# Moving the modulation columns to GpSimd's queue and re-tiling the first output projection

## The chip, the cores and the metric

The kernel runs on one core of a Trainium2 chip. The metric is the device time of one execution, in microseconds (us). Before the change three runs took 2764.96, 2761.36 and 2760.85 us, so the median is 2761.36 us.

A core has a matrix engine (TensorE, PE in the profile; its weight loads are PEld), a vector engine (VectorE, DVE), a scalar engine (ScalarE, ACT), GpSimd (POOL) and a sync engine (SyncE, SP) that issues transfers. Transfers between HBM and the on-chip memory are executed by 16 DMA engines, whoever issued them. Each engine works through its own instructions strictly in order; an instruction that waits holds everything behind it on that engine.

## The reference

Everything is float32, one batch entry, 512 tokens (S), model width 2048 (D). Two layers:

```python
mod = sc @ ada_w[l] + ada_b[l]            # sc = silu(c): one vector of 2048; mod: 3 x 2048 numbers
shift, scale, gate = mod[:, :D], mod[:, D:2*D], mod[:, 2*D:]
h = modulate(rmsnorm(x, g_pre[l]), shift, scale)
y = mlstm_mixer(h, ...)                    # layer 0: 8 heads, width 4096, then @ a_w_out (4096 x 2048)
# layer 1: hkv = modulate(rmsnorm(x, kv_g), ...); kv = hkv @ kv_w; band attention; @ b_w_out
x = x + gate * rmsnorm(y, g_post[l])
```

The `mod` numbers are matrix-vector products. The kernel computes them one "column" at a time: a tile of 128 partitions by 2048 numbers holds the weights of 128 outputs, and one VectorE instruction multiplies it with the broadcast `sc` and sums along the row.

## The kernel before, in words

**Weights.** All weights come as one stream of pieces in a fixed order (`stream`, L75). A piece is a tile of 128 x 1024 numbers, 512 KB. `raw_load` (L223) issues its load on SP into one of three raw buffers; `wpiece` (L232) splits the piece into a rounded part `wh` (a ScalarE copy) and a remainder `wl` (a VectorE subtraction, L213), and the products are made from three matrix multiplications, high x high, high x low, low x high (`mm3`, L280). The raw buffer is free for the next load once `wl` is made. So each piece passes SP, DMA, ScalarE, VectorE and TensorE in turn, with three raw buffers, three of `wh` and three of `wl`.

**Columns.** 32 columns (shift and scale of layer 0) are loaded and summed while the first projections start, on SP's queue. 48 more, 1 MB each, follow in the background while heads 0, 1 and the start of 2 are computed: `background(n)` (L743) first places the sums of the columns loaded by its previous call and then the loads of the next `n`, up to three, in two buffers `ada` of pool `ap_` and one of pool `bp`. Sums and loads are pinned, that is they keep their place in program order on VectorE and on SP. The 32 columns of layer 1's shift and scale come during layer 0's output projection, and the last of them during the key projection, as 64 half columns of 512 KB (`scale_step`, L1096: sums of two halves, then loads of the next two, in two buffers `adh`). They too are on SP's queue, in front of and behind weight pieces.

**Output projection of layer 0.** The result has four token blocks of 128 and four column groups of 512. `rows(g, ms, ...)` (L1065) computes column group `g` for the token blocks `ms`. A piece holds two of the 32 contraction steps of a group; it feeds 2 x 3 matrix multiplications for each token block, so 24 when all four blocks are computed together and 12 when two are. Before, group 0 is computed for all four blocks, then groups 1, 2, 3 for blocks 0 and 1, then groups 1, 2, 3 again for blocks 2 and 3: each of these three groups is loaded and split twice. While blocks 2 and 3 are computed, blocks 0 and 1 are finished: `residual` (L1010) adds the gated result to the input (loads `xr`, stores `xsc`), `turned` (L1030) transposes the normalised rows on TensorE into `ps_x` and stores them to `nsc`; later `kept` (L1056) reads them back from `nsc` and `key_input` (L1022) makes the input `hkv` of the key and value projection.

**Order.** A scheduler orders each engine's instructions by priority (weights are called ahead of their place by `high_priority`), except that pinned instructions stay in program order among themselves.

Of the kernel before, what the change touches and what calls it, by code (L numbers as in the profile page):

```python
# [74 lines left out]
def stream():  # L75
# [30 lines left out]
    for h in range(NH):  # L106
# [50 lines left out]
def hybrid_trunk(ctx, tc, xT, xN, c, adaT, cols, wst, wg, ext, kc, out):  # L157
# [74 lines left out]
    def wpiece(mat, groups=(), pl=None, bufs=(2, 2), early=False):  # L232
# [42 lines left out]
        return out  # L275

    def mm(ps, a, b, start, stop):
        return nc.tensor.matmul(ps, a, b, start=start, stop=stop)  # L278

# [213 lines left out]
    sp = st.enter_context(pool("start"))  # L493
    def ada_load(i, p, n, pin=lambda ins: ins, parts=1, js=None):

        w = D // parts
        js = range(parts) if js is None else js
        at = p.tile([P, w * len(js)], F32, tag="ada", name=f"ada{i}_{js[0]}", bufs=n)
        for j in js:
            c = (j - js[0]) * w  # L500
            pin(nc.sync.dma_start(at[:, c : c + w], adaT[i, :, j * w : (j + 1) * w]))
        return i, at, w, js
# [313 lines left out]
    for h in range(NH):  # L816
# [4 lines left out]
        for i in range(4):  # L821
            if h > HALF:
                if i % 2 == 0:
                    zs = pair((i // 2) * (V0 // 2) + h * DK, f"zq{h}_{i}", BANKS[i // 2])
                ps = zs[i % 2]
            elif h < 2:
                ps = (lead, qk1)[h][i]
            else:
                ps = newp(f"ps_qk{h}_{i}")
                proj_a("a_w_in", h1, ps)  # L830
            qk.append(conv(ps, chs[i], f"{h}_{i}", 1 < h <= HALF))
            if 1 < h <= HALF:
                background(2 - i % 2)
        zs = ps = None
# [52 lines left out]
        if h < HALF:  # L887
            background(2)
        if h:
            so = []  # L890
        for i in range(4):
# [7 lines left out]
            elif h:  # L899
                ps = newp(f"ps_o{h}_{i}")  # L900
                proj_a("a_w_in", h1, ps)
                so.append(acp.tile([P, S], F32, tag="so", name=f"so{h}_{i}", bufs=6))
                nc.scalar.activation(so[i], ps, AF.Sigmoid)
                background(2 - i % 2)
        for i in range(4):
# [41 lines left out]
        if h < HALF:  # L947
            background(3 if h == 0 else 1)
        if h == 3:
# [79 lines left out]

    def turned(pair, gs, use):  # L1030

        ms = PAIRS[pair]
        t = slice(2 * P * pair, 2 * P * (pair + 1))
        for g in gs:
# [5 lines left out]
            for kk in range(2):  # L1040
# [10 lines left out]
                nc.sync.dma_start(nsc[k : k + 2, :, t].rearrange("a p t -> p a t"), keep)  # L1051
                if use:
                    for j in range(2):
                        key_input(k + j, ps[:, j * 2 * P : (j + 1) * 2 * P], t)

# [8 lines left out]

    def rows(g, ms, xs, at={}):  # L1065
        ps = [newp(f"ps_y0_{g}_{m}") for m in ms]
        proj_b("a_w_out", xs, ps, ms=ms, kts=32, at=at)
        with tc.high_priority(AHEAD):
            for p, m in zip(ps, ms):
                yt[m].append(rp.tile([P, S], F32, tag="r", name=f"y{m}_{g}"))  # L1070
                evac(p, m, g, yt[m][g])

    scale_cols = [(48 + i, j) for j in range(2) for i in range(2 * KT)]
    scale_in, scH = [], []

    def scale_sums():

        for i, j, a in scale_in:
            pin(nc.vector.tensor_tensor_reduce(
                a, a, scH[j], 1.0, mod[:, i : i + 1] if j else col(CB + i), ALU.mult, ALU.add, mod[:, i : i + 1]  # L1080
            ))
        scale_in.clear()

    def scale_load():

        for i, j in scale_cols[:2]:
            d = slice(j * 2 * S, (j + 1) * 2 * S)
            if len(scH) == j:
                scH.append(cp.tile([P, 2 * S], F32, tag="sc", name=f"scH{j}"))
                pin(nc.sync.dma_start(scH[j], csc[0, d].partition_broadcast(P)))  # L1090
            a = cp.tile([P, 2 * S], F32, tag="adh", name=f"adh{i}_{j}", bufs=2)
            pin(nc.sync.dma_start(a, adaT[i, :, d]))
            scale_in.append((i, j, a))
        del scale_cols[:2]

    def scale_step():  # L1096
        scale_sums()
        scale_load()

    def scale_steps(*ks):  # L1100
        return {k: scale_step for k in ks}

    gate_row(0, 0)
    rows(0, range(4), y_tile, scale_steps(*range(2, 32, 4)))
    for pair, ms in enumerate(PAIRS):
        for g in range(1, 4):
            at = scale_steps(4, 12, 20, 28) if pair == 0 else {}
            if pair == 1 and g == 1:
                at = {2: lambda: residual(0), 4: lambda: residual(1)}
                at |= {20 + 4 * i: lambda i=i: turned(0, [i], False) for i in range(3)}  # L1110
            if pair == 1 and g == 2:
                at = {2: lambda: turned(0, [3], False)}
            if pair == 1 and g == 3:
                at = {k: lambda k=k: [key_input(i, kept(i, slice(0, 2 * P)), slice(0, 2 * P)) for i in range(k // 2 - 1, k // 2 + 1)] for k in range(2, 32, 4)}
            if pair == 1:
                add_at(at, scale_steps(*((8, 14, 18), (6, 14, 22), ())[g - 1]))
            gate_row(0, g)
            rows(g, ms, ys, at)

# [45 lines left out]
    for pair, ms in enumerate(PAIRS):  # L1165
        for g in range(2):
            turn = {2 + 4 * i: lambda i=i: turned(1, [i], True) for i in range(4)} if pair == 0 and g == 1 else {}
# [19 lines left out]
    assert not scale_cols and not scale_in  # L1187
    zxst.close()
    cqst.close()
    kst.close()  # L1190
# [281 lines left out]
```

## Time and profile before

| what | value |
|---|---|
| median of three runs | 2761.36 us |
| profiled execution | 2767.03 us |
| its span, first to last instruction | 2765.2 us |
| TensorE busy | 2734.7 us |
| VectorE busy | 2320.6 us |
| ScalarE busy | 1437.0 us |
| moved by DMA | 527.25 MB |

How to read it. A busy time counts an instruction from start to end; matrix multiplications overlap, so TensorE reads as busy even in short delays. The window view gives, for a stretch of time, the length, then the busy time and number of instructions of each engine (TensorE, its weight loads, VectorE, ScalarE, GpSimd), the granted TensorE clock, the mean busy share of the 16 DMA engines and the GB/s moved. The view of waits gives who waited for whom: total us, times, longest. The chain view follows the work that ended last back through what released it: start, duration, what. The view of transfers gives the line and tile, number of issues, KB each and the median us from issue to landing.

### The profile page before, as it was taken

Reading aid. Unit: us, or ns where it says so; the run is one execution under the profiler, and the core shown is the slowest. Engines: PE = TensorE matmul, PEld = TensorE weight load, DVE = VectorE, ACT = ScalarE, POOL = GpSimd, SP = SyncE. Lnnn points to the kernel's source line nnn. Section 1 sums busy time; section 2 is a strip of 40 time slices with the busy share of each in tenths; the row PEclk is TensorE's granted clock in tenths of the full one; section 3 lists DMA queues with packets and bytes.
Section 4 is the critical chain, followed back from the end, with each engine's and each line's share of the span. In section 5 each row is a group of like instructions: output and inputs, shape, how many; then the busy total and the mean of one; then the engine's idle time right before and its main releaser. Section 6 shows DMA issues by size and latency. Waiting matters only on the chain.

```text
span 2765.2 us, 45016 instructions
## 1 busy us (share of the span) xinstructions
PE 2734.7 (99%) x17554; PEld 2487.5 (90%) x17554; DVE 2320.6 (84%) x3694; ACT 1437.0 (52%) x2046; POOL 0.2 (0%) x4
## 2 busy tenths in 40 slices
PE   8999999999999999999999999999999999999998
PEld 6887887899999999999998877787998899999887
DVE  8978978989999899998988657667997788899666
ACT  4243523556556565565555234468435566666523
POOL 0000000000000000000000000000000000000000
PEclk9999999999999999999999999999999999999999
DMA  9757787333333233333338778988655544444687
GB/s 368 291 204 275 258 314 255 102 98 120 109 111 113 97 124 108 115 110 100 125 106 284 251 268 293 317 275 279 214 183 187 171 129 129 127 122 126 213 299 256
DMA packets 165296, 527.25 MB, mean 191 GB/s; under 512 B 17701, under 2 KB 33605, under 8 KB 154457
## 3 DMA queue, kind: packets, MB, share of 16 engines
q1 hardware_dynamic: 165082, 524.38, 56.3%
q8 instruction: 137, 2.24, 0.3%
q14 instruction: 77, 0.63, 0.1%
HBM read 490.69 MB, written 38.85 MB: 192 GB/s over the span
## 4 chain that ended last, share of the span: by engine, by line
PE 84%; DMA 7%; DVE 6%; issue 2%; ACT 1%; SPq 0%; DVEq 0%; ACTq 0%
PE ps_y L278 11%; PE ps_azo L278 5%; PE ps_czo L278 5%; PE ps_dzo L278 5%; PE ps_kv L278 4%; PE ps_v L278 4%; PE ps_az L278 3%; PE ps_cz L278 3%; PE ps_dz L278 3%; PE ps_l L278 3%; DMA wr<-in_wst 3%; PE ps_bzo L278 3%; PE ps_o L278 3%; PE ps_s L278 2%; PE ps_czq L278 2%; PE ps_cv L278 2%
## 5 line engine op out<-in xcount | busy, mean ns | idle before, releaser
L213 ACT CAST wh<-wr 128x1024 fp32r<-128x1024 f32 (+1 forms) x560 | 579.2, 1036 | 563.7 <-PE ps_y L278 159.8
L213 DVE TENSOR_TENSOR wl<-wr,wh 128x1024 fp32r<-128x1024 f32 (+1 forms) x560 | 671.2, 1203 | 164.8 <-ACT wh L213 163.4
L278 PE MATMUL ps_y<-wh,y 128*128 128x512 f32 x1536 | 478.0, 391 | 0.2 <-ACT sqy L1000 0.2
L213 ACT CAST wsh<-ws 128x768 fp32r<-128x768 f32 (+1 forms) x272 | 222.5, 818 | 406.1 <-issue 128.7
L278 PEld LDWEIGHTS ps_y<-wh,y 128*128 128x128 f32 x1536 | 288.9, 188 | 60.5 <-ACT sqy L1000 0.6
L213 DVE TENSOR_TENSOR wsl<-ws,wsh 128x768 fp32r<-128x768 f32 (+1 forms) x272 | 253.8, 933 | 91.0 <-ACT wsh L213 88.3
L278 PE MATMUL ps_y<-wl,y 128*128 128x512 f32 x768 | 301.7, 393 | 5.4 <-DVE wl L213 5.3
L507 DVE CUSTOM_DVE_ANT_0 ada<-ada,scB,cl 128x2048 f32<-128x2048 f32 (+1 forms) x80 | 185.2, 2319 | 22.8 <-DMA ada<-in_adaT 22.6
L252 DVE TENSOR_TENSOR ws<-wr 128x512 f32<-128x512 f32 (+1 forms) x272 | 181.0, 670 | 2.7 <-DMA wr<-in_wst 2.6
L278 PEld LDWEIGHTS ps_y<-wl,y 128*128 128x128 f32 x768 | 144.7, 188 | 41.8 <-DVE wl L213 12.1
L278 PE MATMUL ps_kv<-wh,hkv 128*128 128x512 f32 x512 | 159.6, 391 | 0.5 <-ACT wh L213 0.5
L278 PE MATMUL ps_v<-wh,h 128*128 128x512 f32 x384 | 120.2, 390 | 0.0
L278 PEld LDWEIGHTS ps_kv<-wh,hkv 128*128 128x128 f32 x512 | 96.1, 188 | 20.6 <-ACT wh L213 0.9
L254 DVE TENSOR_TENSOR ws<-wr 128x256 f32<-128x256 f32 (+1 forms) x272 | 111.0, 413 | 3.0
L253 DVE TENSOR_TENSOR wr<-ws,wr 128x256 f32<-128x256 f32 (+1 forms) x272 | 110.5, 411 | 1.9
L278 PE MATMUL ps_kv<-wl,hkv 128*128 128x512 f32 x256 | 100.0, 391 | 1.1 <-DVE wl L213 1.1
L278 PE MATMUL ps_l<-h,wh 128*128 128x512 f32 x320 | 98.4, 390 | 0.0
L278 PEld LDWEIGHTS ps_v<-wh,h 128*128 128x128 f32 x384 | 72.0, 188 | 14.8
L278 PE MATMUL ps_azo<-h,wh 128*128 128x256 f32 (+1 forms) x404 | 82.1, 294 | 0.0
L278 PE MATMUL ps_v<-wl,h 128*128 128x512 f32 x192 | 75.1, 391 | 0.0
L278 PEld LDWEIGHTS ps_l<-h,wh 128*128 128x128 f32 x320 | 59.9, 188 | 12.7 <-ACT wh L213 0.3
L278 PE MATMUL ps_dzo<-h,wh 128*128 128x256 f32 x364 | 69.6, 283 | 0.0
(442 smaller groups left out, 7219.4 us busy)
## 6 DMA issues: line engine op xcount, KB each, us to landing
wr<-in_wst SPq DMA_DIRECT2D x530, 512.0 KB, 3.9
ada<-in_adaT SPq DMA_DIRECT2D x78, 1024.0 KB, 7.1
adh<-in_adaT SPq DMA_DIRECT2D x64, 512.0 KB, 5.5
ada<-in_adaT SPq DMA_DIRECT2D x36, 512.0 KB, 6.1
xt<-nsc SPq DMA_DIRECT2D x48, 256.0 KB, 3.9
wr<-in_wst SPq DMA_DIRECT2D x26, 384.0 KB, 3.9
yr<-ysc SPq DMA_DIRECT2D x28, 256.0 KB, 5.3
ysc<-zo SPq DMA_DIRECT2D x24, 256.0 KB, 4.0
```

Of the source, the lines that this page charges most:

```text
L213: ins = nc.scalar.copy(hi, src), nc.vector.tensor_tensor(lo, src, hi.bitcast(F32), op=ALU.subtract)
L252: nc.vector.tensor_tensor(t[:, : 2 * w], r[:, w : 3 * w], r[:, : 2 * w], op=ALU.subtract)
L253: nc.vector.tensor_tensor(r[:, w : 2 * w], t[:, w : 2 * w], r[:, :w], op=ALU.add)
L254: nc.vector.tensor_tensor(t[:, 2 * w :], r[:, 3 * w :], r[:, w : 2 * w], op=ALU.subtract)
L278: return nc.tensor.matmul(ps, a, b, start=start, stop=stop)
L507: pin(nc.vector.tensor_tensor_reduce(c, c, (sc or scB)[:, j * w : (j + 1) * w], 1.0, mod[:, i : i + 1] if j else col(CB + i), ALU.mult, AL ...
```

## The change

1. `ada_load` takes the queue as an argument. `background` now issues its loads on GpSimd's queue, fills up to three loads on every call, and sums the `n` oldest instead of all; its calls are spread differently over heads 0 and 1. The 64 half columns move to GpSimd's queue too, with three buffers in place of two, three at a time.
2. A background sum is still pinned, and besides is placed behind the matrix multiplication that was last written when the call was made (`paced`). This is an ordering for the scheduler, and no wait on the chip.
3. The output projection of layer 0 computes groups 0 and 1 for all four token blocks, then groups 2 and 3 for blocks 0 and 1, then groups 2 and 3 for blocks 2 and 3. The stream has six groups of 16 pieces in place of seven.
4. The residual of blocks 0 and 1 is made during group 2 of the second pair, and all of `turned` during its group 3, where it makes the key input directly from `ps_x`. Reading it back from `nsc` falls away.
5. All half columns are summed by the end of the output projection, none in the key projection. The result tiles of group 3 of the first pair lie in the pool `tp`, of six buffers.

```diff
-    tile_b("a_w_out", 0, 32)
-    for _ in PAIRS:
-        for g in range(1, 4):
-            tile_b("a_w_out", g * 512, 32)
+    for g in (0, 1, 2, 3, 2, 3):
+        tile_b("a_w_out", g * 512, 32)
...
+    def paced(ins):
+        behind(ins, product[0])
+        return pin(ins)
+
     def background(n):
-        for a in loaded:
-            ada_sum(*a, tc.keep_in_program_order)
-        loaded.clear()
-        for b, i in enumerate(pending[:n]):
-            loaded.append(ada_load(i, *((ap_, 2) if b < 2 else (bp, 1)), tc.keep_in_program_order))
-        del pending[:n]
+        for a in loaded[:n]:
+            ada_sum(*a, paced)
+        del loaded[:n]
+        while pending and len(loaded) < 3:
+            p, bufs = (bp, 1) if len(pending) % 3 == 0 else (ap_, 2)
+            loaded.append(ada_load(pending.pop(0), p, bufs, pin, queue=nc.gpsimd))
...
-                background(2 - i % 2)
+                background(2)
...
-            add_at(at, {k: lambda: background(2) for k in ((2, 4, 6, 8, 10, 12, 14) if h == 0 else (2, 6, 12))})
+            add_at(at, {k: lambda: background(2) for k in ((0, 4, 8, 12) if h == 0 else (2, 6, 10, 14))})
...
+    def half_sums_step():
+        for i, j, a, w in halves:
+            paced(nc.vector.tensor_tensor_reduce(
+                a, a, w, 1.0, mod[:, i : i + 1] if j else col(CB + i), ALU.mult, ALU.add, mod[:, i : i + 1]
+            ))
+        halves.clear()
+        while cols_left and len(halves) < 3:
+            i, j = cols_left[0]
+            d = slice(j * 2 * S, (j + 1) * 2 * S)
...
+            a = cp.tile([P, 2 * S], F32, tag="adh", name=f"adh{i}_{j}", bufs=3)
+            pin(nc.gpsimd.dma_start(a, adaT[i, :, d]))
+            halves.append((i, j, a, sc[1]))
+            cols_left.pop(0)
...
     gate_row(0, 0)
-    rows(0, range(4), y_tile, scale_steps(*range(2, 32, 4)))
+    rows(0, range(4), y_tile, steps_at(*range(4, 32, 4)))
+    gate_row(0, 1)
+    rows(1, range(4), ys, steps_at(*range(0, 32, 4)))
     for pair, ms in enumerate(PAIRS):
-        for g in range(1, 4):
...
+        for g in (2, 3):
+            if pair == 0:
+                at = steps_at(*((4, 14, 24), (2, 12, 22))[g - 2])
+            elif g == 2:
+                at = {2: lambda: residual(0), 6: lambda: residual(1), 14: half_sums_step, 24: half_sums_step}
+            else:
+                at = {6 + 6 * i: lambda i=i: turned(0, [i]) for i in range(4)}
             gate_row(0, g)
-            rows(g, ms, ys, at)
+            rows(g, ms, ys, at, tp if pair == 0 and g == 3 else None)
...
-        if 0 < i < 7:
-            at[1] = scale_step
-        if i == 7:
-            at[1] = lambda: (scale_sums(), amul_cols(2, 48 + KT, GPRE + KT))
```

More of the change, by code (lines that the diff above doesn't have):

```diff
@@ L275, in wpiece @@
         return out
+    product = [None]
     def mm(ps, a, b, start, stop):
-        return nc.tensor.matmul(ps, a, b, start=start, stop=stop)
+        product[0] = nc.tensor.matmul(ps, a, b, start=start, stop=stop)
+        return product[0]
     def mm3(ps, ah, al, bh, bl, start, stop):
@@ L493, in hybrid_trunk, with ada_load @@
     sp = st.enter_context(pool("start"))
-    def ada_load(i, p, n, pin=lambda ins: ins, parts=1, js=None):
+    def ada_load(i, p, n, pin=lambda ins: ins, parts=1, js=None, queue=nc.sync):
         w = D // parts
@@ L500, in ada_load @@
             c = (j - js[0]) * w
[L501 removed]
+            pin(queue.dma_start(at[:, c : c + w], adaT[i, :, j * w : (j + 1) * w]))
         return i, at, w, js
@@ L1028, in key_input, with turned @@
         split(hkv[k][:, 0, t], hkv[k][:, 1, t], tmp)
-    def turned(pair, gs, use):
+    def turned(pair, gs):
         ms = PAIRS[pair]
@@ L1051, in turned @@
                 nc.sync.dma_start(nsc[k : k + 2, :, t].rearrange("a p t -> p a t"), keep)
-                if use:
-                    for j in range(2):
-                        key_input(k + j, ps[:, j * 2 * P : (j + 1) * 2 * P], t)
+                for j in range(2):
+                    key_input(k + j, ps[:, j * 2 * P : (j + 1) * 2 * P], t)
     def kept(k, t):
@@ L1063, in hybrid_trunk, with rows @@
     yt = [[] for _ in range(4)]
-    def rows(g, ms, xs, at={}):
+    def rows(g, ms, xs, at={}, pl=None):
         ps = [newp(f"ps_y0_{g}_{m}") for m in ms]
@@ L1069, in rows @@
             for p, m in zip(ps, ms):
-                yt[m].append(rp.tile([P, S], F32, tag="r", name=f"y{m}_{g}"))
+                yt[m].append((pl or rp).tile([P, S], F32, tag="t" if pl else "r", name=f"y{m}_{g}"))
                 evac(p, m, g, yt[m][g])
[L1073 to L1080, printed above, removed]
-            ))
-        scale_in.clear()
@@ L1084, in scale_load @@
-    def scale_load():
-        for i, j in scale_cols[:2]:
+    cols_left = [(48 + i, j) for j in range(2) for i in range(2 * KT)]
+    halves, sc = [], [None, None]
+    def half_sums_step():
+        for i, j, a, w in halves:
+            paced(nc.vector.tensor_tensor_reduce(
+                a, a, w, 1.0, mod[:, i : i + 1] if j else col(CB + i), ALU.mult, ALU.add, mod[:, i : i + 1]
+            ))
+        halves.clear()
+        while cols_left and len(halves) < 3:
+            i, j = cols_left[0]
@@ L1103, in hybrid_trunk, with steps_at @@
+    def steps_at(*ks):
+        return {k: half_sums_step for k in ks}
     gate_row(0, 0)
-    rows(0, range(4), y_tile, scale_steps(*range(2, 32, 4)))
+    rows(0, range(4), y_tile, steps_at(*range(4, 32, 4)))
+    gate_row(0, 1)
+    rows(1, range(4), ys, steps_at(*range(0, 32, 4)))
     for pair, ms in enumerate(PAIRS):
-        for g in range(1, 4):
[L1107 to L1116, printed above, removed]
+        for g in (2, 3):
[5 more added lines that the diff above has]
+                at = {6 + 6 * i: lambda i=i: turned(0, [i]) for i in range(4)}
@@ L1117, in hybrid_trunk @@
             gate_row(0, g)
-            rows(g, ms, ys, at)
+            rows(g, ms, ys, at, tp if pair == 0 and g == 3 else None)
+    assert not cols_left and not halves
+    amul_cols(2, 48 + KT, GPRE + KT)
+    cqst.close()
     def values(g, ms, at={}):
@@ L1166, in hybrid_trunk @@
         for g in range(2):
-            turn = {2 + 4 * i: lambda i=i: turned(1, [i], True) for i in range(4)} if pair == 0 and g == 1 else {}
+            turn = {2 + 4 * i: lambda i=i: turned(1, [i]) for i in range(4)} if pair == 0 and g == 1 else {}
             if pair:
```

25 lines of the change are left out of this document (8 added, 17 removed).

## The prediction

> **What bounds the kernel now.** I read the page's shares first, then the chain of work that ended last, then the window view of the stages that the chain leaves TensorE in, then the waits inside them.
>
> ```profile
> span 2765.2 us, 45016 instructions
> PE 2734.7 (99%) x17554; PEld 2487.5 (90%) x17554; DVE 2320.6 (84%) x3694; ACT 1437.0 (52%) x2046; POOL 0.2 (0%) x4
> ...
> PE 84%; DMA 7%; DVE 6%; issue 2%; ACT 1%; SPq 0%; DVEq 0%; ACTq 0%
> ```
>
> TensorE is the bound, and the change takes no matrix multiplication away. What can be won is where the chain leaves TensorE. It does so in the start, at the end of head 1 (between us 366 and 425) and in the output projection of layer 0 (us 1557 to 1757). GpSimd does nothing: its queue is free.
>
> The next rows are windows of the output projection, counting `ps_y` products alone (length, busy and count, clock, DMA share, GB/s); the fourth is a window of all engines at the end of head 1, the fifth of the key projection.
>
> ```profile
> 1556.78:1699.00 142.22, 137.03 (x587) 1.00 0.79 271
> 1699.00:1757.11 58.11, 52.85 (x220) 0.97 0.91 305
> 1757.11:1841.46 84.35, 84.35 (x372) 1.00 0.87 293
> 366.00:425.00 59.00, 55.12 (x249) 46.28 (x248) 44.91 (x44) 16.46 (x21) 0.00 (x0) 0.97 0.84 305
> 1930.00:2097.00 167.00, 166.95 (x1338) 164.11 (x1337) 155.25 (x263) 72.54 (x91) 0.00 (x0) 1.00 0.58 189
> ```
>
> The third row is undisturbed: 84.35 / 372 = 0.2267 us per product. At that pace the 587 products of the first row need 133.1 of 142.2 us: TensorE lost 9.1 us there (blocks 0 and 1, groups 1 to 3). In the second row 220 products need 49.9 us, and 32 transposes run there too, which take 0.88 / 8 = 0.11 us each (row below), 3.5 us: 4.7 us lost. The fourth row loses 59.00 - 55.12 = 3.9 us. These 17.7 us are all that parts 1 to 4 below can win.
>
> How the 9.1 us come about shows one turn of the chain (start, duration, what):
>
> ```profile
> 1590.15 6.52 DMA wr<-in_wst
> 1596.77 1.06 ACT wh L213
> 1597.85 0.15 DVE wl L213
> 1598.00 0.99 issue
> 1598.99 0.27 DVE adh L1079
> 1599.26 0.93 issue
> 1600.19 0.08 DVE mod L1079
> 1600.28 1.20 DVE adh L1079
> 1601.48 1.15 DVE wl L213
> 1602.65 6.70 DMA wr<-in_wst
> ...
> 1747.07 0.88 PE ps_x L1046 x8
> ```
>
> A piece lands, is rounded, gets its remainder; two column sums follow on VectorE; the next remainder frees a raw buffer, and only then can SP ask for the next piece. The turn takes 1602.65 - 1590.15 = 12.50 us and brings four pieces, which TensorE uses up in 4 x 12 x 0.2267 = 10.88 us. The first row holds 587 / 48 = 12.2 turns; 9.1 / 12.2 is 0.75 us lost in each, after what the buffers cover.
>
> **The change part by part.** Transfers in that stretch, and the waits of SP and VectorE (rows of the waits: the first three of us 1557 to 1757, the others of us 237 to 425):
>
> ```profile
> wr<-in_wst SPq DMA_DIRECT2D x47, 512.0 KB, 5.7
> adh<-in_adaT SPq DMA_DIRECT2D x24, 512.0 KB, 6.1
> ...
> SPq L1092 <- DVE mod L1079: 27.0, 23, 2.6
> DVE adh L1079 <- DMA adh<-in_adaT: 6.7, 8, 1.7
> DVE y L1017 <- DMA xr<-in_xN: 2.5, 1, 2.5
> ...
> SPq L501 <- DVE mod L507: 82.5, 27, 6.3
> DVE ada L507 <- DMA ada<-in_adaT: 19.8, 15, 3.8
> PE ps_n L278 <- DVE so L934: 3.9, 1, 3.9
> ```
>
> *1. Group 1 for all four blocks.* Sixteen pieces of 512 KB, with a ScalarE copy of 1.06 and a remainder of 1.20 us each (the mean of the row below), fall away. None of that is on TensorE, so I cost it at nothing by itself. But a piece of group 1 now feeds 24 products, 5.44 us, and group 0, which runs so already, has a stretch without loss:
>
> ```profile
> 1487.80 68.96 PE ps_y L278 x304
> ...
> L213 DVE TENSOR_TENSOR wl<-wr,wh 128x1024 fp32r<-128x1024 f32 (+1 forms) x560 | 671.2, 1203 | 164.8 <-ACT wh L213 163.4
> ```
>
> So 32 pieces of the 48 stay in the narrow form. *2. Half columns on GpSimd, three at a time.* In the changed order of VectorE's instructions a turn is five pieces and three sums; one of the three sums stands one remainder later. Its longest path is one landing, one copy (1.06), three remainders (3.6) and two sums (2.5, from the turn above): landing + 7.2 us, against 5 x 2.72 = 13.6 us of TensorE. It keeps up while pieces land within 6.4 us; before, it was 5.7 in the median, with half columns in front on the same queue. SP no longer waits for VectorE to free a column buffer (27.0 us in that stretch). I take 0.25 us per turn over six turns, 1.5 us left of 9.1: **-7.6**. Bounds: nothing left (-9.1), or the same loss per piece on two thirds of the pieces (6.1 left, -3.0).
>
> *3. The second pair.* Here the chain ran through one `xr` load of 5.55 and one half column of 7.58 us, with VectorE waiting:
>
> ```profile
> 1719.16 5.55 DMA xr<-in_xN
> ...
> 1729.63 7.58 DMA adh<-in_adaT
> ...
> 1738.98 0.98 PE ps_x L1046 x7
> ```
>
> The transposes come a group later, when `xn` is long ready, and two steps of half columns are left there. But of the eight `xr` loads, before mostly asked for far ahead, all now stand among the weights on SP, and a store `xsc` behind each waits for VectorE with pieces queued behind it: eight loads of 5.5 us, about half of them one after the other, take some 30 us beside the 11 pieces between them, 30 us. That is even. I leave 3.2 of 4.7: **-1.5**; bounds -4.7 and +3 (two of the eight loads fully shown, 11.0 us, less the three pieces of 2.72 us that the buffers hold). Making `hkv` from `ps_x` drops 16 loads of 128 KB (row below) and adds nothing but a longer hold of `ps_x`: nothing, as TensorE asks for the next one 8 us later.
>
> *4. Background columns of heads 0 to 2.* At the end of head 1 VectorE waited for columns (19.8 us over heads 0 and 1), because a load could start only after the sum before it, and SP stood behind it for 82.5 us. Three in flight on a free queue start a call earlier, 48 products or 10.9 us ahead, against a landing of 7.1:
>
> ```profile
> ada<-in_adaT SPq DMA_DIRECT2D x33, 1024.0 KB, 7.1
> ...
> xt<-nsc SPq DMA_DIRECT2D x16, 128.0 KB, 4.5
> ```
>
> Without these waits VectorE reaches `so` before TensorE needs it: **-3.9**. Bound: 0, since head 1 now moves 28 columns where it moved 23, at a DMA share of 0.84 already.
>
> *5. The first of them starts at time zero.* On SP it stood behind all loads of the start. On GpSimd nothing stands ahead of it, and its buffer in `bp` was never used before: in the changed order this load waits for nothing. It is 1.05 MB among the start's loads, where the engines are full:
>
> ```profile
> 0.00:5.00 5.00, 2.55 (x3) 1.15 (x4) 0.18 (x3) 1.76 (x2) 0.20 (x4) 1.00 0.38 118
> 5.00:10.00 5.00, 4.61 (x6) 1.31 (x4) 1.18 (x2) 3.83 (x6) 0.00 (x0) 1.00 1.01 420
> 25.00:30.00 5.00, 5.00 (x18) 3.41 (x17) 4.93 (x7) 1.87 (x3) 0.00 (x0) 1.00 1.03 416
> 45.00:50.00 5.00, 4.86 (x21) 3.67 (x20) 4.96 (x7) 1.14 (x2) 0.00 (x0) 1.00 0.97 357
> ...
> 25.78 2.18 PE L278 MATMUL ps_lead<-h,wh 128*128 128x512 f32 x5
> ```
>
> At 420 GB/s it takes 2.5 us; a part may fall into the first microseconds, where the engines still idle (0.38). VectorE is full from us 25 on (4.93 of 5.00), so the delay isn't caught up. I take **+2.0**, bounds 0 and +2.5.
>
> *6. No sums in the key projection.* TensorE had 166.95 of 167.00 us there: nothing.
>
> **The sum** against the profiled execution (2767.03 us): -7.6 - 1.5 - 3.9 + 2.0 = -11.0, so 2756.0. The median of the three runs lies 5.7 us below that execution; with the same difference the forecast is 2761.4 - 11.0 = **2750.4 us**. The lower bounds sum to -9.1 - 4.7 - 3.9 + 0 = -17.7 (2743.7), the upper to -3.0 + 3 + 0 + 2.5 = +2.5 (2763.9).
>
> **The rivals.** *A: the DMA engines are the limit, not the order on a queue.* The stretches run at shares of 0.79 to 0.91, so pieces land as late as before from whatever queue. Then 6.1 of 9.1 us stay, the second pair and head 1 keep theirs, and the start loses 2.0: -3.0 + 2.0 = -1.0, 2760.4. For it speaks the share; against it that before, even the undisturbed third window had 0.87. The Trainium skill, page "DMA: Bandwidth & Descriptors", section "Issuing engines are not separate DMA queues", states this rival's rule: all queues run on the same 16 engines, and a second one saves only the sequencer's time. Chance 0.15.
>
> *B, slower: three columns in flight hold the pieces up.* On one queue at most two half columns stood before a piece; now three alternate with it. If they all go first, 3 x 0.52 MB at the 420 GB/s of the start add 3.7 us to the 3.9 that a piece takes on the whole page, 7.6. Each us over 6.4 costs 1 us per turn. It decides where it makes good all gains: 6 x (landing - 6.4) - 9.1 + 2.0 = 5.5 at a landing of 8.5 us; at 9 us, with nothing won in head 1 and the second pair, it is 15.6 - 9.1 + 2.0 = +8.5, 2770. Chance 0.13.
>
> ```profile
> wr<-in_wst SPq DMA_DIRECT2D x530, 512.0 KB, 3.9
> ```
>
> *C, slower: columns issued by GpSimd land late, because GpSimd is held up while VectorE runs.* The pinned sum then waits on VectorE with remainders behind it. Up to 10.9 us a landing costs nothing; beyond that head 1 loses its gain and more, I put +6, 2767. No run before has such a load, and nothing here speaks for a hold-up. The page "SBUF — State Buffer", section "SBUF: two separate sides", of the Trainium skill warns of it for copies and tensor-scalar forms in the two-port mode; by the same page a tensor-tensor has no such mode, and remainders are of that form. Chance 0.04.
>
> **How the numbers follow.** 0.2% is 5.5 us, about what a measurement of this kernel can tell from no change. The forecast with its bounds holds 0.68; nearly all of that is under 2755.9. Rival A is "no change", B and C are slower. So faster 0.66, same 0.17, slower 0.17. The likeliest case alone spans 2743.7 to 2756; for 8 in 10 the range must reach over rival A to the upper sum: 2743 to 2764.
>
> **What would show it.** Right: `wr` still in the order of 5 us in the groups of pairs, no turn of the chain through `DMA wr` there, the groups 0 and 1 at 0.2267 us per product; no wait of `ps_n` for `so` at the end of head 1; the first product of `ps_lead` some 2 us later than 25.78. Wrong: pieces landing over 6.4 us beside the half columns, VectorE waiting for `adh` or `ada`, SP waiting for `xsc` in the second pair, or a start that isn't delayed.

## The result, and the profile after

The changed kernel takes 2771.41 us (median of 20 runs, 2762.96 to 2777.75), the kernel before, on the same chip, 2762.1 us (20 runs, 2758.2 to 2767.12). The ratio is 1.0030, with a 95% interval of 1.0023 to 1.0038: the change made the kernel 8 to 9 us slower. The forecast was 2750.4 us, and faster.

The page of the profiled execution after (2771.67 us, close to the median):

```profile
span 2769.9 us, 44953 instructions
PE 2732.5 (99%) x17554; PEld 2485.8 (90%) x17554; DVE 2303.5 (83%) x3678; ACT 1419.1 (51%) x2030; POOL 60.6 (2%) x118
...
q1 hardware_dynamic: 143914, 428.68, 46.2%
q0 software_dynamic: 16416, 84.94, 8.8%
```

The last two rows are DMA queues (packets, MB, share of the 16 engines' time): SP's, and GpSimd's, which now carries 84.94 MB. TensorE is the bound as before, so I cut the execution into four stages by its instructions (timeline of one tile on TensorE: count, ns, first and last start):

```profile
L278 PE MATMUL ps_lead<-h,wh x192: 387/389/521, 27.7 to 182.8; 128*128 128x512 f32 x192
...
L278 PE MATMUL ps_y<-wh,y x1536: 387/389/505, 1469.2 to 2761.4; 128*128 128x512 f32 x192
...
L278 PE MATMUL ps_kv<-wh,hkv x512: 387/389/477, 1846.3 to 2188.2; 128*128 128x512 f32 x171
```

The start is the time to the first `ps_lead`; the heads reach from there to the first `ps_y`, the output projection of layer 0 from there to the first `ps_kv`, and the rest to the last `ps_y`. The table has these four for every kernel of this study ("before, again" is a second profiled execution of the unchanged kernel). Ratios are to the kernel before on the same chip; 0.001 is 2.8 us. The stages come from one profiled execution each: 2767.03 us for the kernel before, which is near the top of its 20 runs, and 2766.74, 2766.95 and 2766.49 us for e1, e2 and e3, which is 3 to 7 us under their medians.

| kernel | time | ratio [95%] | start | heads | projection | rest |
|---|---|---|---|---|---|---|
| before | 2762.1 | 1 | 25.8 | 1444.5 | 371.0 | 915.3 |
| before, again | 2759.8 | (one run) | 25.7 | 1442.5 | 368.5 | 912.7 |
| changed | 2771.4 | 1.0030 [1.0023, 1.0038] | 27.7 | 1441.5 | 377.1 | 915.1 |
| e1 first column on SP | 2771.4 | 1.0026 [1.0017, 1.0035] | 26.0 | 1439.6 | 376.5 | 913.9 |
| e2 first batch on SP | 2774.3 | 1.0033 [1.0022, 1.0045] | 27.9 | 1440.7 | 374.3 | 913.5 |
| e3 `xr` on GpSimd | 2770.0 | 1.0024 [1.0013, 1.0035] | 28.2 | 1441.2 | 373.6 | 913.2 |
| e123 all three | 2768.0 | 1.0017 [1.0008, 1.0026] | 25.6 | 1445.7 | 373.0 | 914.9 |
| d1 heads' half, GpSimd | 2764.8 | 1.0009 [1.0000, 1.0017] | 27.7 | 1442.9 | 368.8 | 914.3 |
| d4 heads' half, SP | 2760.6 | 0.9991 [0.9982, 1.0000] | 25.8 | 1439.7 | 371.5 | 914.2 |
| d2 projection's half, GpSimd | 2766.0 | 1.0014 [1.0004, 1.0023] | 25.9 | 1441.2 | 376.8 | 914.0 |
| d5 projection's half, SP | 2755.3 | 0.9971 [0.9959, 0.9983] | 25.8 | 1442.7 | 360.3 | 917.2 |
| d3 both halves, SP | 2751.4 | 0.9955 [0.9943, 0.9967] | 25.7 | 1439.1 | 362.9 | 913.3 |
| g1 = d3, halves on GpSimd | 2767.1 | 1.0014 [1.0004, 1.0023] | 25.8 | 1439.0 | 376.5 | 915.2 |
| g2 = d3, halves later, ScalarE | 2757.1 | 0.9979 [0.9971, 0.9988] | 25.7 | 1438.9 | 369.2 | 913.5 |
| g3 = d3, halves later, SP | 2751.6 | 0.9956 [0.9943, 0.9968] | 25.7 | 1439.6 | 362.1 | 914.0 |
| g4 = d3, halves later, GpSimd | 2766.1 | 1.0011 [1.0001, 1.0021] | 25.6 | 1439.2 | 378.2 | 913.4 |
| h1 = g4, gated | 2760.2 | 0.9991 [0.9982, 1.0000] | 25.7 | 1439.0 | 373.2 | 912.7 |

Of the changed kernel's stages the projection is the one that went wrong: 377.1 us where 371.0 and 368.5 stood before. It loses in three places. At its beginning, where the chain is

```profile
1466.30 10.52 DMA yr<-ysc
...
1477.46 0.51 ACT dd L927
...
1478.01 3.43 PE ps_n L278 x11
1481.44 9.32 PE ps_y L278 x41
```

a load of y lands after 10.52 us. GpSimd's timeline tells what goes beside it: the first scale row and three half columns, 2 MB, sent off as soon as GpSimd's wait for them was over, 3.5 us before the first `ps_y` product. (The brackets give how long the engine had been idle, and what ended that.)

```profile
1465.73 0.53 POOL L1097 DMA_DIRECT2D scH<-csc  x1 [992.57 <-DMA wr<-in_wst]
1466.28 1.64 POOL L1099 DMA_DIRECT2D adh<-in_adaT  x3
```

Second, in groups 2 and 3 of the first pair the chain runs through weight pieces again, and third, in group 2 of the second pair, through the loads `xr`, each behind a store that waits for VectorE:

```profile
1661.53 6.81 DMA wr<-in_wst
...
1679.03 6.96 DMA wr<-in_wst
...
1758.65 0.33 SPq L1025
...
1759.02 5.49 DMA xr<-in_xN
...
1764.54 0.76 DVE y L1023
1765.31 0.33 SPq L1025
...
1765.69 5.51 DMA xr<-in_xN
```

### The profile page after: what moved, and what is told of

Its sections match the earlier page's. It is cut to its first block, busy times and chain, and to the rows that moved or that the text cites. A ratio compares the mean times of both kernels' runs of the same rounds, so it can differ in the third digit from the quotient of the medians.

```text
span 2769.9 us, 44953 instructions
## 1 busy us (share of the span) xinstructions
PE 2732.5 (99%) x17554; PEld 2485.8 (90%) x17554; DVE 2303.5 (83%) x3678; ACT 1419.1 (51%) x2030; POOL 60.6 (2%) x118
## 3 DMA queue, kind: packets, MB, share of 16 engines
q0 software_dynamic: 16416, 84.94, 8.8%
## 4 chain that ended last, share of the span: by engine, by line
PE 80%; DMA 6%; issue 6%; DVE 6%; ACT 1%; POOL 0%; SPq 0%; DVEq 0%; ACTq 0%; POOLq 0%
PE ps_y L278 13%; PE ps_azo L278 5%; PE ps_czo L278 5%; PE ps_dzo L278 5%; PE ps_kv L278 4%; PE ps_az L278 3%; PE ps_cz L278 3%; PE ps_dz L278 3%; PE ps_l L278 3%; PE ps_bzo L278 3%; DMA wr<-in_wst 3%; PE ps_czq L278 2%; PE ps_cv L278 2%; PE ps_dzq L278 2%; PE ps_azq L278 2%
## 5 line engine op out<-in xcount | busy, mean ns | idle before, releaser
L211 ACT CAST wh<-wr 128x1024 fp32r<-128x1024 f32 (+1 forms) x544 | 562.7, 1036 | 568.7 <-PE ps_y L278 206.1
L211 DVE TENSOR_TENSOR wl<-wr,wh 128x1024 fp32r<-128x1024 f32 (+1 forms) x544 | 652.9, 1203 | 176.9 <-ACT wh L211 174.7
```

The costliest lines, as they stand in the source:

```text
L211: ins = nc.scalar.copy(hi, src), nc.vector.tensor_tensor(lo, src, hi.bitcast(F32), op=ALU.subtract)
```

## The experiments

My first theory was that each place has its own cause, an order of DMA issues that can be mended there: the first column (2 us), the first batch beside y (4.8 us), the `xr` loads on SP (4 to 8 us). The rival was that lost time comes back elsewhere.

**e1, the first background column on SP's queue.**

```diff
-            loaded.append(ada_load(pending.pop(0), p, bufs, pin, queue=nc.gpsimd))
+            q = nc.sync if len(pending) == len(cols_left) else nc.gpsimd
+            loaded.append(ada_load(pending.pop(0), p, bufs, pin, queue=q))
```

> The changed kernel with one edit: the first background column is loaded by SP's queue, in its place among the first loads, all others by GpSimd's. Theory A (a GpSimd load has no place in SP's order and starts at time zero beside the first pieces of xt): the first leading product comes 2 us earlier than in the changed kernel (27.7 to about 25.7 us) and the time falls by 2 us, to about 2769.4 us against 2771.4. Theory B (the start is as late for another reason): the first leading product stays at 27.7 us and the time stays within 0.5 us of 2771.4.

The start is back at 26.0 us, so the first column was the cause of its 2 us. The time, 2771.44 us, shows no gain that could be told from none.

**e2, the first batch of half columns on SP's queue**, in `half_sums_step`:

```diff
+            q = nc.sync if len(cols_left) > 61 else nc.gpsimd
...
-                pin(nc.gpsimd.dma_start(sc[1], csc[0, d].partition_broadcast(P)))
+                pin(q.dma_start(sc[1], csc[0, d].partition_broadcast(P)))
...
-            pin(nc.gpsimd.dma_start(a, adaT[i, :, d]))
+            pin(q.dma_start(a, adaT[i, :, d]))
```

> The changed kernel with one edit: the first batch of half columns (one scale row and three half columns, 2 MB) is loaded by SP's queue, behind the loads of y, and not by GpSimd's as soon as its buffers come free. Theory A (the 2 MB beside the loads of y make them land in 10.5 us and not 5.1): the loads of y land in 5 to 6 us again, the first products of the output projection's tail come 4 to 5 us earlier, and the time falls by 4 to 5 us, to about 2767 us. Theory B (the loads of y are slow because the stores of y just before are late): landing stays near 10 us and the time stays within 1 us of 2771.4.

The beginning was mended (y lands in 5.5 us in the median), but the projection's stage is only 2.8 us shorter, 374.3 us, and the time isn't lower at all, 2774.25 us. In the trace the first pair, from the start of its first product to the start of the second pair's, takes 95.7 us where the changed kernel took 93.6; but e1, whose projection is the changed kernel's, has 95.8 there, so it isn't shown that the loss moved from the beginning to the pairs.

**e3, the loads `xr` of the first pair on GpSimd's queue.**

```diff
-            nc.sync.dma_start(xr, xN[m, :, d])
+            (nc.gpsimd if m < 2 else nc.sync).dma_start(xr, xN[m, :, d])
```

> The changed kernel with one edit: the eight loads xr of the first pair's residual step are issued by GpSimd's queue and not by SP's, so that none stands behind a store of xsc that waits for VectorE. Theory A (the loads of xr go one after the other because each stands on SP behind the store of the block before, and the pieces of the weights stand behind them): the second pair's first column group loses 4 to 5 us and not 9.2, as before the change, and the time falls by 4 to 5 us, to about 2767 us. Theory B (the DMA engines are the limit there, so the order of the issues gives nothing): the loss stays within 1.5 us of 9.2 and the time within 1.5 us of 2771.4.

**e123, the three edits together.**

> The changed kernel with all three edits: first background column on SP's queue, first batch of half columns on SP's queue, loads xr of the first pair on GpSimd's queue. Theory A (three separate losses of 2, 4.8 and 4 to 5 us from the order of the DMA issues): they add up, the time falls by 10 to 12 us, to 2759 to 2762 us, at or just below the kernel before. Theory B (the lost time is given back later, as the same bytes have to pass the same DMA engines): the sum is under half of that, 2766 us or more.

2769.95 and 2767.96 us: e3 stays within theory B's 1.5 us, and e123 won 3.5 of the 10 to 12 us, as its theory B said. Theory A fell, as a sum of three places. So I took the change apart, by halves and by queues.

**The kernel before again; the two halves of the change alone; the change with all loads on SP.** d1 takes the new `background` and its calls, d2 the new projection with its half columns. d3 is the changed kernel with this edit:

```diff
-            loaded.append(ada_load(pending.pop(0), p, bufs, pin, queue=nc.gpsimd))
+            loaded.append(ada_load(pending.pop(0), p, bufs, pin, queue=nc.sync))
...
-                pin(nc.gpsimd.dma_start(sc[1], csc[0, d].partition_broadcast(P)))
+                pin(nc.sync.dma_start(sc[1], csc[0, d].partition_broadcast(P)))
...
-            pin(nc.gpsimd.dma_start(a, adaT[i, :, d]))
+            pin(nc.sync.dma_start(a, adaT[i, :, d]))
```

> The kernel before, unchanged, for a second profile, which tells how much one stage moves from one execution to the next. Theory A (the stages repeat to within 1 us and only the total of the first profile is high): the stage from the first scores' key product to the first product of the output projection's tail takes 1048.1 us again, the output projection's two pairs 371.0 us again, and one other stage is 2 to 5 us shorter. Theory B (a stage varies by itself): the stage of the first head's gates and columns, 396.4 us in the first profile, is 391 to 398 us.

> The kernel before with the change's first half alone: the background columns by GpSimd's queue, three under way, with the new numbers of columns at each place; the output projection as before. Theory A (the profiles' stages: start +2.0 us, first head -2.9 us, rest as before): within 1.5 us of the kernel before, 2761 to 2764 us. Theory B (the 9 us between the medians come from this half, by the transfers beside head 0 and head 1): 2768 us or more.

> The kernel before with the change's second half alone: the output projection's new order and its half columns by GpSimd's queue; the background columns of the heads by SP's queue as before. Theory A (the loss is made in the output projection, 371.0 to 377.1 us between the profiles): 5 to 9 us slower than the kernel before, 2768 to 2772 us. Theory B (the loss is made in the heads): within 2 us of the kernel before.

> The changed kernel with every load that it gave to GpSimd's queue on SP's queue, in program order, three under way as in the change. Theory A (the separate queue is at fault, as its loads start beside the critical ones, +2.0 us at the start and +4.8 us at the beginning of the output projection): 4 to 7 us faster than the changed kernel, 2764 to 2767 us. Theory B (a load on SP that waits for its buffer, held by a sum on VectorE, holds up the pieces of the weights behind it): slower than the changed kernel, by 2 us or more.

d1 is 1.8 us slower than the kernel before on its chip, just over theory A's 1.5. d2 is 2.9 us slower, between its two theories. d3 takes 2751.35 us, 0.45% less than the kernel before and 20 us less than the changed one: more than theory A gave the queue, and no sign of theory B. The same tiling, the same three columns under way, the same bytes, and only the queue differs. The second profile of the kernel before shows how far a stage moves by itself: the heads by 2.0, the projection by 2.5 us, more than theory A's 1 us.

d3 is the fastest version, with g3 below. The next windows start in each kernel 186.2 us after its first `ps_y` product and last 86.3 us (`ps_y` products alone: TensorE, its weight loads, VectorE, ScalarE, clock, DMA share, GB/s). In the changed kernel, the first row, they hold groups 2 and 3 of the first pair; d3, the second, is further on, and its last 55 products belong to the second pair.

```profile
1655.40:1741.70 86.30, 82.78 (x353) 65.39 (x353) 1.28 (x2) 1.30 (x4) 1.00 0.79 272
```

```profile
1651.00:1737.30 86.30, 86.07 (x380) 70.94 (x379) 2.56 (x4) 2.59 (x8) 1.00 0.87 302
```

In the same time TensorE does 380 products in place of 353; 27 x 0.2267 is 6.1 us. The DMA engines are busier in d3, not less busy. So it isn't the DMA engines' capacity that limits the changed kernel here. The waits of SP's queue in d3, us 1651 to 1747:

```profile
SPq L227 <- DVE wl L211: 44.7, 33, 2.7
SPq L227 <- DMA wr<-in_wst: 10.3, 6, 2.8
SPq L1099 <- DVE mod L1086: 8.7, 11, 0.9
```

SP does wait for VectorE to free the buffers of half columns, 8.7 us in 11 times, and TensorE loses nothing by it. In the heads, us 370 to 425, the changed kernel (first row) loses 2.0 us and d3 (second) nothing. There the DMA engines are fuller in the changed kernel, 0.98 of the time, so this window doesn't tell the queue from the engines as the limit.

```profile
370.00:425.00 55.00, 53.00 (x245) 44.32 (x244) 48.81 (x47) 15.06 (x19) 7.41 (x14) 1.00 0.98 370
```

```profile
370.00:425.00 55.00, 55.00 (x256) 46.28 (x255) 45.55 (x47) 16.30 (x20) 0.00 (x0) 1.00 0.86 332
```

**Which queue, and when.** The next four start from d3. g1 puts the half columns back on GpSimd. g2, g3 and g4 issue each batch later, four contraction steps after its sums (two in groups 0 and 1), on ScalarE's, SP's and GpSimd's queue:

```diff
         halves.clear()
+    def half_loads_step():
         while cols_left and len(halves) < 3:
...
-    def steps_at(*ks):
-        return {k: half_sums_step for k in ks}
+    def steps_at(*ks, lag=4):
+        return {k: half_sums_step for k in ks} | {k + lag: half_loads_step for k in ks}
```

> The all-SP version with one edit: the half columns of the output projection by GpSimd's queue again, the background columns of the heads stay on SP's. Theory A (in the projection a second queue's pieces are moved between the weight pieces that TensorE waits for; that made 14.2 of the 20.4 us between the profiles of the changed kernel and the all-SP version): 10 to 15 us slower than the all-SP version, 2761 to 2766 us. Theory B (most of the loss comes from the heads' columns on the second queue): within 5 us of the all-SP version, 2751 to 2756 us.

> The all-SP version with the half columns issued by ScalarE's queue, each batch of three four positions later than the sums that free its buffers (two in the first two column groups), so that ScalarE does not wait long for VectorE. Theory A (any second queue beside SP's costs, as its pieces are moved between the weights'): as slow as with GpSimd's queue in the same places, 2760 us or more. Theory C (only GpSimd's kind of queue costs): within 3 us of the same version on SP's queue.

> The control for the runs with later loads: the same later places, on SP's queue. Both theories: 2750 to 2756 us, as the loads still land (6 us) before their sums (about 13.6 us after the last ones); if it is above 2758 us the later place costs by itself.

> The same later places, on GpSimd's queue. Theory D (the queue costs nothing, only the moment at which it bursts, right as the buffers come free): within 3 us of the same version on SP's queue. Theories A and C (a second queue costs wherever it is issued): 2760 us or more.

g1 says that most of the 20 us, 15.7, come from the half columns in the projection. g3 is as fast as d3. g2 lies between: 5.5 us over the same on SP, which is neither theory A's "as slow as GpSimd's" nor theory C's "within 3 us". It brings a wait of its own, though. ScalarE also makes the copies `wh`, and in g2 these stood behind loads that waited for the sums (us 1650.8 to 1746.8; d3 has no such row):

```profile
ACT wh L211 <- DVE mod L1086: 14.4, 7, 3.0
```

So g2 doesn't tell what a second queue costs by itself. g4 did not do what it was meant to. GpSimd has nothing else to do, so a later place in the program isn't a later issue:

```profile
1461.30 0.66 POOL L1099 DMA_DIRECT2D scH<-csc  x1 [1460.85 <-DMA wr<-in_wst]
1461.95 1.56 POOL L1101 DMA_DIRECT2D adh<-in_adaT  x3
```

The loads go off beside the critical y as in the changed kernel. So theory D was still open, and h1 gives GpSimd something to wait for.

**h1, g4 gated.** `product[1]` is the last weight operand, the newest `wh`; the loads behind the copy are `paced` too.

```diff
     def half_loads_step():
+        gate = cp.tile([P, 1], F32, tag="gate", name=f"gate{len(cols_left)}")
+        paced(nc.gpsimd.tensor_copy(gate, product[1][:, 0:1].bitcast(F32)))
         while cols_left and len(halves) < 3:
```

> The half columns by GpSimd's queue in the later places, as in the run before, but now each batch of three stands on GpSimd behind a copy of one column of the newest weight piece's wh, so that it can't be issued before ScalarE has got that far. (In the run with later places GpSimd, which has nothing else to do, still issued them the moment their buffers came free: 1461.30 us for the first.) Theory D (the loss is made by the moment of the issue): as with ScalarE's queue in the same places or better, 2757 us or less, and the first products of the projection's tail lose 1 us and not 4. Theory C (GpSimd's kind of queue costs whenever it issues): 2763 us or more.

**d4 and d5, the halves of the change alone with all loads on SP.**

> The kernel before with the change's first half alone (three background columns under way, the new numbers at each place), all on SP's queue; the output projection as before. Theory A (this half is worth what the stage before the first scores' key product shows, 422.2 and 420.2 us in two profiles of the kernel before, 416.6 us in the all-SP version): 3 to 6 us faster than the kernel before, and 4 to 8 us faster than the same half on GpSimd's queue. Theory B (the queue makes no difference in the heads): within 1.5 us of the same half on GpSimd's queue, 2763 to 2766 us.

> The kernel before with the change's second half alone, its half columns on SP's queue; the heads as before. Theory A (the two halves on SP's queue add up: 11.7 us for both, 2.0 us for the heads' half): about 10 us faster than the kernel before, 2752 to 2754 us. Theory B (the projection's new order gains only when the heads' columns come in time too): 6 us faster at most, 2757 us or more.

h1 takes 2760.16 us, between the two theories: the gate wins back 5.9 of g4's 14.5 us over g3, and 8.5 stay. But the gate delayed only the first batch. GpSimd's timeline in h1, at the beginning and in the first pair, and a row of the waits (us 1650.9 to 1746.9):

```profile
1461.91 1.24 POOL L1093 COPY gate<-wh 128x1 f32<-128x1 f32 x1 [1461.46 <-ACT wh L211]
1463.09 0.66 POOL L1101 DMA_DIRECT2D scH<-csc  x1
...
1662.89 1.17 POOL L1093 COPY gate<-wh 128x1 f32<-128x1 f32 x1 [8.47 <-ACT wh L211]
1665.63 0.54 POOL L1103 DMA_DIRECT2D adh<-in_adaT  x1 [1.57 <-DVE mod L1086]
...
POOL adh L1103 <- DVE mod L1086: 22.8, 17, 1.8
```

The first batch starts 1.8 us later than in g4. In the pair the copy is done before the sums are, and the loads still go off as soon as the sums free their buffers, as in g4. The later places of g2 and g3 delay nothing there either: their loads go off 0.04 us after the sums (in g3 every third after 1.55 us). So in the pairs theory D's later issue was tried by no version. The stretch of the first pair still loses where d3's doesn't (windows of all engines, 96 us; h1, g2, d3 in this order):

```profile
1650.90:1746.90 96.00, 90.65 (x385) 71.01 (x384) 59.56 (x74) 35.39 (x41) 14.84 (x22) 1.00 0.78 270
```

```profile
1650.80:1746.80 96.00, 93.50 (x402) 74.38 (x400) 61.87 (x76) 36.87 (x43) 0.00 (x0) 1.00 0.81 283
```

```profile
1651.00:1747.00 96.00, 95.77 (x423) 78.96 (x422) 65.67 (x80) 40.35 (x49) 0.00 (x0) 1.00 0.88 303
```

d4 and d5 are 2.0 and 7.3 us faster than the kernel before, together 9.4 of d3's 11.7, so by the intervals they add up. For d5 theory A asked for 2752 to 2754 and got 2755.26. The same halves on GpSimd's queue, d1 and d2, are 1.8 and 2.9 us slower than the kernel before.

## Why the prediction was wrong

**What failed** is the price of the other queue, which the sum put at nothing. In step 2 the queue was only a gain ("SP no longer waits for VectorE to free a column buffer"), in step 4 "a free queue". Two things were missing. At the beginning of the projection it is the moment: SP's queue keeps the first half columns behind y (in d3 the first is issued 19.9 us after the first `ps_y` product), GpSimd's sends them 2.9 us before it. In the pairs it is the second queue itself, for the moment is the same there: in the first pair of d3 a half column's load is issued 0.04 us after the sum that frees its buffer (every third 1.55 us), in the changed kernel 0.41 us after. Still TensorE loses 0.2 us there in d3 and 6.3 in the changed kernel (step 2 below). What the second queue does to the pieces is read from one turn. GpSimd issued three half columns (its timeline):

```profile
1659.56 0.53 POOL L1099 DMA_DIRECT2D adh<-in_adaT  x1 [13.07 <-DVE mod L1086]
1660.77 0.53 POOL L1099 DMA_DIRECT2D adh<-in_adaT  x1 [0.68 <-DVE mod L1086]
1663.11 0.53 POOL L1099 DMA_DIRECT2D adh<-in_adaT  x1 [1.81 <-DVE mod L1086]
```

and SP weight pieces from 1661.53 on (the chain above); two of them fall before us 1665. Transfers from us 1661.6 to 1665.0, and from 1665.0 to 1669.0:

```profile
q0 software_dynamic: 215, 0.82, 86.8%
q1 hardware_dynamic: 3, 0.01, 0.6%
...
q1 hardware_dynamic: 231, 0.88, 54.8%
q0 software_dynamic: 185, 0.65, 43.3%
```

For 3.4 us next to nothing of the pieces is moved (0.01 MB), and then the rest of the three half columns, of which the third was issued after the first piece, takes 0.65 of 1.53 MB beside them. That piece landed after 6.81 us. Part of the 3.4 us is the usual start: in d3 a piece issued while SP's queue moved nothing had its first packet 0.95 to 1.14 us later (232 pieces). In the changed kernel 14 of 263 such pieces took over 1.5 us, the longest 4.46. The Trainium skill, page "DMA: Bandwidth & Descriptors", section "Queues, rings and completion order", says that each DMA engine goes round between the queues that have work, packet by packet; the second window agrees with it (54.8 and 43.3%). The first window isn't explained by it.

**Step 1** was right: groups 0 and 1 run without loss after the first ten microseconds (778 x 0.2267 = 176.4 us in the second row; windows of all engines of the changed kernel, from its first `ps_y` on).

```profile
1469.20:1479.20 10.00, 6.40 (x30) 5.13 (x30) 5.88 (x10) 6.30 (x11) 0.00 (x0) 0.92 1.01 385
1479.20:1655.40 176.20, 176.20 (x778) 146.13 (x777) 118.26 (x158) 54.10 (x75) 22.21 (x42) 0.99 0.76 257
```

**Step 2** forecast 1.5 us left of 9.1 as long as pieces land within 6.4 us. By products (353 x 0.2267 = 80.0 of 86.3 us) 6.3 us are lost in the changed kernel, with landings of 6.5 us in the median; on SP it is 0.2 us (380 x 0.2267 = 86.1) with 5.8:

```profile
wr<-in_wst SPq DMA_DIRECT2D x30, 512.0 KB, 6.5
adh<-in_adaT POOLq DMA_DIRECT2D x18, 512.0 KB, 6.7
```

```profile
wr<-in_wst SPq DMA_DIRECT2D x31, 512.0 KB, 5.8
adh<-in_adaT SPq DMA_DIRECT2D x17, 512.0 KB, 6.4
```

The limit of 6.4 us was hardly passed in the median, but the pieces on the chain took 6.81, 6.96 and 7.20 us. So the re-tiling and three columns at a time win the loss back, but on SP's queue, which the step thought in their way; which of the two does it was not tried apart. The 9.1 us were themselves high: in the second profile of the kernel before the same 576 products, 130.6 us of work, take 136.6 us, 6.0 us lost. **Step 3** forecast 3.2 us left of 4.7. Group 2 of the second pair, its 192 products from first to last, the changed kernel and then d3 (`ps_y` alone; a window counts products cut by its edges too):

```profile
1746.30:1798.90 52.60, 46.18 (x193) 35.51 (x193) 1.28 (x2) 1.29 (x4) 1.00 0.85 275
```

```profile
1731.60:1780.50 48.90, 44.40 (x194) 35.76 (x192) 1.28 (x2) 1.30 (x4) 1.00 0.87 287
```

192 products are 43.5 us: 9.1 and 5.4 lost. The eight `xr` loads weren't "even" (the step's "some 30 us" for half of eight loads of 5.5 us is not worked out either, half of them are 22): on SP's queue alone they cost the 1.5 us that the step hoped to win and 0.7 more, and with the last half columns on the other queue another 3.7, beyond the step's bound of +3. That it is these loads rests on the chain, and on e3's trace, where this group takes 49.6 us. **The beginning of the projection** stood in no step. Step 5 saw that a GpSimd load is held by nothing at time zero, but not that the first batch of half columns is in the same position beside y. There TensorE gets to 30 matrix multiplications in the first 10 us (first row of step 1) where d3 does 49: 4.3 us.

```profile
1464.80:1474.80 10.00, 9.41 (x49) 7.84 (x48) 8.45 (x15) 9.20 (x17) 0.00 (x0) 1.00 1.03 372
```

**Step 4** (-3.9) holds on SP's queue: the stage of the heads is 1439.1 us in d3, 1444.5 and 1442.5 before, and d4 is 2.0 us faster (0 to 5 by its interval). On GpSimd's queue most of it is gone in d1: 1442.9 us, and the start pays 2; the changed kernel's 1441.5 us is 3.0 or 1.0 less than before, by the profile it is held against. **Step 5** (+2.0) was right in the trace, 27.7 us and with e1 26.0.

Put together, from the first profile of the kernel before to the changed kernel's (2767.03 to 2771.67 us, +4.6), with TensorE's losses in the projection counted over 0.2267 us a product between the starts of the stages' first products: step 2 gave -2.8 for -7.6, step 3 +4.2 for -1.5, the beginning +4.8 for nothing, step 4 -3.0 for -3.9, step 5 +1.9 for +2.0; the rest is 0.2 us shorter. So steps 2 and 3 are mis-sized by 4.8 and 5.7 us, and the beginning is a term that the sum lacks. Against the second profile of the kernel before the whole projection is 8.6 us longer, and the heads 1.0 us shorter.

**The rivals.** A, that the DMA engines are the limit from whatever queue, falls in the projection with d3, which is faster there at a higher share of them (0.87 against 0.79); in the heads, where the changed kernel's share was 0.98, it isn't excluded. The Trainium skill's rule that stood beside it (page "DMA: Bandwidth & Descriptors", section "Issuing engines are not separate DMA queues": a second issuing engine saves no more than its sequencer's time) is right in that nothing is gained, but here the second engine cost 15.7 us for the half columns (g1 against d3). B, that three columns in flight hold the pieces up, named the mechanism of the first pair, but it isn't the three: d3 has them too. It needs the second queue. That B's 2770 us lies near the measured time is luck: it stands on landings of 9 us, and they were 6.5. C, a hold-up of GpSimd by VectorE, doesn't show in the changed kernel: each issue of a half column takes 0.53 us, and they wait for the sums that free their buffers.

**How close the number was to d3.** The sum of -11.0 comes near the version with all loads on SP's queue (-11.7), since steps 2 and 4 were sized by buffers and turns, not by the queue. It is partly luck: the sum holds +2.0 for the start, which d3 doesn't pay, and -1.5 for the second pair, which d3 doesn't win. The forecast's mistake is one of cause: it counted the other queue among the gains, and the queue lost them.

**What stays open.** Of g4's 14.5 us over g3, 5.9 are the moment at which the first batch is issued (g4 against h1): in the first 10 us of the projection TensorE does 33 matrix multiplications in g4 and 51 in h1, which is 4.1 us. The other 8.5 us remain in h1 with the loads of the pairs issued as their buffers come free. On SP's queue they are issued no later (d3, g3), so the moment doesn't make this loss; whether a later issue on GpSimd's queue would avoid it was not tried. How the second queue makes it is read from the one turn above, from the first packets and from the landings, not from a run of its own. ScalarE's queue in the same places costs 5.5 us, of which the part that its own waits for the sums make is not known; so it isn't settled whether GpSimd's kind of queue costs more than another. And e2's time isn't explained: its trace is 2.8 us shorter in the projection, but it is of the fastest of its six runs.

## What to carry to other kernels

A queue that looks like a bottleneck because it waits may be what keeps the critical loads first. Before loads are moved to an idle engine's queue, ask for each of them when its buffer comes free and which load will be under way then: an idle engine issues at that moment, whatever its place in the program. And test a change of queue apart from a change of tiling, since here one hid the gain of the other. A version that is meant to issue later has to be checked in its trace for when it does issue.

## What was not expected of the hardware

- In the windows of the first pair the DMA engines were busy for 0.87 of the time from one queue in d3 (302 GB/s), and for 0.78 to 0.81 from two in the changed kernel, g2 and h1 (270 to 283 GB/s), with TensorE waiting for pieces only in the second case. The share alone tells little: the kernel before had 0.79 from one queue, and lost too.
- Two pieces issued on SP's queue while a batch from GpSimd's was under way got 0.01 MB moved in 3.4 us.
- The queue of SP costs little where it waits: 8.7 us of waits for column buffers in d3, with TensorE at 86.07 of 86.30 us.
